# The last two GLA heads of a hybrid layer: matrix times activations first, then the value weights

## The chip, the cores and the metric

The kernel runs on one core of a Trainium2 chip. The metric is the device time of one launch in microseconds (us). The core has five engines that run side by side, each with an order of instructions fixed beforehand: TensorE (PE; its weight loads are listed as PEld), VectorE (DVE), ScalarE (ACT), GpSimd (POOL) and SyncE (SP), which here only issues transfers. They wait for one another by semaphores.

## The reference, cut to what matters

The layer works on 256 latent tokens and 256 context tokens of width 2048, in fp32. One input projection feeds windowed attention (16 query heads, 4 key heads), gated linear attention (GLA, 4 heads), and two gates. Only what the change touches:

```python
h = modulate(x, g_mix, shift, scale)     # rms_norm(x) * g * (1 + scale) + shift; the context likewise
qa, ka, va, qb, kb, vb, rb, lrf, lrb, gate_a, gate_b = split(h @ w_in)
# GLA, per head: a token's output is a sum over all tokens s, of latent and context,
#   o[t] = sum_s A[t, s] * vb[s]
# A comes from qb, kb and the decays alone; vb = h @ w_in[:, VB + 512*head : ...]
y_att = o_attn @ w_attn_o
y_gla = (rms_norm(o_gla, gla_norm) * silu(rb)) @ w_gla_o
x = x + mod * ((sigmoid(gate_a) * y_att + sigmoid(gate_b) * y_gla) @ w_out)
```

Since vb = h W, the output A vb can be formed as A (h W) or as (A h) W.

## The kernel before, in words

**Products.** Every large fp32 product is made of three fast ones: each factor is split into a high and a low part, and high × high, low × high and high × low are summed in a PSUM bank. `split` copies the high part on ACT (L62) and subtracts on DVE (L63). Weights stream as 512 KB pieces (two blocks of 128 rows by 512 columns) through SP's queue into seven `raw` buffers; `wsplit` splits each into `whi` (ACT, L220) and `wlo` (DVE, L221), three buffers each. A projection of 512 columns (`proj_nat`, `proj_T`) has eight such pieces. One piece costs TensorE 12 products of 512 columns where the 256 latent tokens alone are projected, and 24 for all 512 tokens.

**Order.** A scheduler fixes the order on each engine. In the code, `tick()` runs once a piece: it runs what `defer(n, ...)` put off by n pieces, advances a generator in `beside`, and runs steps of `bg_steps` at the rate `bg_rate`. Those steps make the later modulation vectors, each with one 512 KB load and one DVE instruction (L403).

**The stages that matter.** Four blocks with a GLA matrix beside them: `with_gla(h, ...)` runs `gla_A(h, ...)`, which yields the split matrices `ats` (latent) and `atc` (context), beside a block: the second half of the keys for head 0, the values of head 1, 2 and 3 (`v_block`, 192 products of 512 columns each) for the others. `gla_o(h, ...)` then multiplies matrix and values (24 products of 512 into `po`) and leaves the output in `og`, its sums of squares in `ssg`. For h > 0 `gla_A` uses split factors (`q2s`, `q3s`, `kk`) for the context's matrix, for h = 0 fp32 ones (`kf`, `kg`).

Then come attention's keys (KA) and values (VA) with `bg_rate` 1.6, and with `bg_rate` 0 the four query blocks (`qa_block`). `attend(g)` runs beside query block g + 1, the last one beside the first gate block (GA, into `m1`). In attention, `norm_rope` scales the queries by `rms_scale`, which is an Ln (L440) and an Exp (L441) on ACT with a Newton step on DVE around them (L442 to L445). Transposes put the queries into `ptq` and, split, into `qT`; `pS` holds scores, L1121 masks them into `s` and takes the maximum `mx`; the exponentials are transposed (`ptp`), split (`pth`, `ptl`) and multiplied by the values into `poa`. Banks `ptq`, `pS`, `ptp`, `poa`, `po` and others share a few PSUM banks, three of them "side" banks.

After attention `rg = rms_scale(ssg, ...)` scales the GLA outputs, four blocks `rb` are made with `bg_rate` 0.62, and the merge follows. Its Sigmoid of the gate `m1` (in `at_evac`, for j = 0, L1221) needs only `m1`. ACT computes a function from the table of a set that is loaded (ACT_TABLE_LOAD); early in the kernel a set that holds both Ln and Exp is loaded.

Of the kernel before, what the change touches and what calls it, by code (L numbers as in the profile page):

```python
# [32 lines left out]
def layer_kernel(ctx, tc, A, out):  # L33
# [27 lines left out]
    def split(hi, lo, src):  # L61
        S.activation(hi, src, AF.Copy)  # L62
        return V.tensor_tensor(lo, src, hi.bitcast(F32), op=ALU.subtract).ins  # L63
# [737 lines left out]
    def gla_A(h, kb, qb, R, gc, res):  # L801
# [44 lines left out]
        def products(lv, q2, k2):  # L846
            pa = bank("pa", (P, 2, P), side=True)
            for t in range(2):
                tq = t if lv < 7 else 1 - t
                for dt in range(2):  # L850
                    mm_b(pa[:, t, :], k2[:, dt, t * P:(t + 1) * P],
                              q2[:, dt, tq * P:(tq + 1) * P], start=(dt == 0), stop=(dt == 1))
            if lv < 7:
                V.copy_predicated(at, lmask[:, lv:lv + 1, :].to_broadcast([P, 2, P]), pa)
            else:
                split(ats[0][:, 0], ats[0][:, 1], at)
                split(ats[1][:, 0], ats[1][:, 1], pa)
# [187 lines left out]
    def norm_rope(b, r, t, tag, fold=None):  # L1045

        y = W2(tag, "y", [P, 4, P])
        S.activation(y, b.rearrange("p (h d) -> p h d", h=4), AF.Copy)
        sq = W2("fc", "sq", [P, 512])
        S.activation(sq, y.rearrange("p h d -> p (h d)"), AF.Square)  # L1050
        s4 = sm.tile([P, 4], F32, name="s4", tag="s4")
        V.tensor_reduce(s4, sq.rearrange("p (h d) -> p h d", h=4), op=ALU.add, axis=AX.X)
# [16 lines left out]

    kTh, kTl = M("kTh", [P, 4, 512], F32R), M("kTl", [P, 4, 512], F32R)  # L1070

    def ka_evac(i, b):
        z = norm_rope(b, rk if i < 2 else None, i % 2, "fa")

        def turn():
            pt = bank("ptk", (P, 4, P))
            for h in range(4):
                turn_b(pt[:, h, :], z[:, h, :], ident)
            split(kTh[:, :, i * P:(i + 1) * P], kTl[:, :, i * P:(i + 1) * P], pt)

        defer(2 + i, turn)
# [26 lines left out]
    def attend(g, qT, qr):  # L1108
        for t in range(2):
# [4 lines left out]
            for h in range(4):  # L1114
                qh, ql = (qT[:, i, h, t * P:(t + 1) * P] for i in range(2))
                pS = bank("pS", side=True)
                mm_b(pS, qh, kTh[:, g, :], start=True, stop=False)
                mm_b(pS, qh, kTl[:, g, :], start=False, stop=False)
                mm_b(pS, ql, kTh[:, g, :], start=False, stop=True)
                s_ = W2("fa", "s", [P, 512])  # L1120
                V.tensor_tensor_reduce(out=s_, in0=pS, in1=amask[:, t, :], scale=1.0, scalar=NEG,  # L1121
                                       op0=ALU.add, op1=ALU.max, accum_out=mx[:, h:h + 1])
                sc.append(s_)
# [42 lines left out]
    bg_rate[0] = 0.0  # L1166
    qTs = qa_block(0)
    m1 = [[W2("fc", "m1", [P, 512]) for _ in range(2)]]

    def ga_block():  # L1170
        proj_nat(w_in, 0, GA, ALL, h_x, lambda t, b: S.activation(m1[0][t], b, AF.Copy))

    for g in range(4):
        beside[:] = [attend(g, *qTs), 0.7, -2.9]
        qTs = qa_block(g + 1) if g < 3 else ga_block()
        for _ in beside[0]:
            pass
        beside.clear()
# [14 lines left out]
    for j in range(4):  # L1193
        def rb_evac(t, b, j=j):
# [278 lines left out]
```

## Time and profile before

| | |
|---|---|
| time, median of 3 runs | 1956.05 us (1956.04 to 1956.2) |
| time of the profiled execution | 1956.3 us, its span 1954.5 us |
| granted TensorE clock | 1.00 of full speed |
| transfers | 420.85 MB, mean 215 GB/s |
| ACT_TABLE_LOAD | 10, of 1283 ns |

A group in the profile reads: line, engine, operation, output<-inputs, shape, count; then busy time in us, mean ns of one; then the idle time of the engine just before. A timeline row reads: start in us, length in us, engine, line, operation, and in brackets the idle time before it with what ended it. A row of waits has total us, times, longest us.

### The profile page before, as it was taken

The numbers are of one execution on the slowest core, as the hardware profiler recorded it, in microseconds if no ns is written. First come the engines' busy times: TensorE is split into PE (matmuls) and PEld (weight loads), VectorE is DVE, ScalarE is ACT, GpSimd is POOL, SyncE is SP. The second block draws the span as 40 slices with busy tenths as digits, with TensorE's granted clock in tenths as the row PEclk, the third lists the DMA queues.
The fourth block names the chain that finished last, engine by engine and source line by source line (L and its number), as shares of the span: only waits on it lengthen the run. The fifth ranks groups of instructions, "written<-read, shape, count | busy, mean of one in ns | idle before, by whom it ended". The sixth has DMA issues, their size and how long they took to land.

```text
span 1954.5 us, 26414 instructions
## 1 busy us (share of the span) xinstructions
PE 1940.3 (99%) x9956; PEld 1612.6 (83%) x9956; DVE 1400.5 (72%) x2165; ACT 985.8 (50%) x1426; POOL 44.9 (2%) x60
## 2 busy tenths in 40 slices
PE   8999999999999999999999999999999999999999
PEld 6678888888887788888888888888888888888887
DVE  5756867785768898777775467998886555777754
ACT  5223666642355665444444445855555334655533
POOL 0010011110000000000000000000000000000000
PEclk9999999999999999999999999999999999999999
DMA  9984222236553467898987777688886666666663
GB/s 396 412 301 141 76 65 65 76 116 225 183 173 107 126 216 255 291 312 302 311 309 231 237 258 240 194 277 286 267 286 217 193 193 185 192 186 193 193 213 111
DMA packets 182576, 420.85 MB, mean 215 GB/s; under 512 B 12480, under 2 KB 12704, under 8 KB 177200
## 3 DMA queue, kind: packets, MB, share of 16 engines
q1 hardware_dynamic: 180912, 413.45, 64.8%
q0 software_dynamic: 1360, 5.54, 0.9%
q8 instruction: 78, 1.28, 0.3%
q14 instruction: 50, 0.41, 0.1%
q10 hardware_dynamic: 176, 0.17, 0.0%
HBM read 416.98 MB, written 2.13 MB: 214 GB/s over the span
## 4 chain that ended last, share of the span: by engine, by line
PE 96%; DMA 3%; ACT 1%; DVE 1%; issue 0%; POOL 0%; SPq 0%; ACTq 0%; DVEq 0%
PE acc L84 74%; PE accs L84 12%; PE pa L96 2%; PE poa L96 1%; PE pS L96 1%; PE po L96 1%; DMA mraw<-in_w_mod 1%; PE pm L96 1%; PE ptp L99 1%; DMA xr<-in_ctxT 1%; DMA raw<-in_w_in 1%; PE pto L99 0%; DMA pack<-in_k_pack 0%; PE plr L646 0%; PE ptx L99 0%; PE pr L491 0%
## 5 line engine op out<-in xcount | busy, mean ns | idle before, releaser
L220 ACT ACTIVATE whi<-raw 128x1024 fp32r<-128x1024 f32 x568 | 601.4, 1060 | 760.5 <-PE acc L84 594.5
L221 DVE TENSOR_TENSOR wlo<-raw,whi 128x1024 fp32r<-128x1024 f32 x568 | 693.4, 1223 | 399.7 <-ACT whi L220 386.1
L84 PE MATMUL accs<-h,whi 128*128 128x512 f32 x704 | 244.5, 392 | 0.0
L84 PE MATMUL acc<-h,whi 128*128 128x512 f32 x640 | 222.3, 392 | 0.0
L84 PE MATMUL accs<-h,wlo 128*128 128x256 f32 x704 | 196.0, 278 | 0.0
L84 PE MATMUL acc<-h,wlo 128*128 128x256 f32 x640 | 178.1, 278 | 0.0
L84 PEld LDWEIGHTS accs<-h,whi 128*128 128x128 f32 x704 | 131.8, 187 | 29.9
L84 PEld LDWEIGHTS acc<-h,whi 128*128 128x128 f32 x640 | 119.8, 187 | 27.0
L84 PE MATMUL acc<-whi,ah 128*128 128x512 f32 x352 | 137.1, 389 | 0.0
L84 PE MATMUL acc<-whi,al 128*128 128x512 f32 x352 | 137.0, 389 | 0.0
L84 PEld LDWEIGHTS accs<-h,wlo 128*128 128x128 f32 x704 | 132.5, 188 | 0.0
L84 PEld LDWEIGHTS acc<-h,wlo 128*128 128x128 f32 x640 | 120.5, 188 | 0.1
L84 PE MATMUL acc<-whi,h2hi 128*128 128x512 f32 x256 | 101.3, 396 | 0.0
L84 PE MATMUL acc<-whi,h1hi 128*128 128x512 f32 x256 | 100.8, 394 | 0.0
L84 PE MATMUL acc<-whi,h0hi 128*128 128x512 f32 x256 | 100.5, 392 | 0.0
L84 PE MATMUL acc<-whi,h0lo 128*128 128x512 f32 x256 | 100.2, 391 | 0.0
L84 PE MATMUL acc<-whi,h3hi 128*128 128x512 f32 x256 | 99.9, 390 | 0.0
L84 PE MATMUL acc<-whi,h1lo 128*128 128x512 f32 x256 | 99.9, 390 | 0.0
L84 PE MATMUL acc<-whi,h2lo 128*128 128x512 f32 x256 | 99.8, 390 | 0.0
L84 PE MATMUL acc<-whi,h3lo 128*128 128x512 f32 x256 | 99.7, 390 | 0.0
L84 PE MATMUL acc<-wlo,ah 128*128 128x512 f32 x352 | 94.2, 389 | 0.0
L403 DVE CUSTOM_DVE_ANT_0 raw<-raw,csrow,pack 128x1024 f32<-128x1024 f32 x64 | 81.3, 1280 | 0.0
(396 smaller groups left out, 3498.2 us busy)
## 6 DMA issues: line engine op xcount, KB each, us to landing
raw<-in_w_in SPq DMA_DIRECT2D x204, 512.0 KB, 4.6
raw<-in_w_up SPq DMA_DIRECT2D x176, 512.0 KB, 4.4
raw<-in_w_modT SPq DMA_DIRECT2D x128, 512.0 KB, 4.5
raw<-in_w_down SPq DMA_DIRECT2D x88, 512.0 KB, 3.7
mraw<-in_w_mod SPq DMA_DIRECT2D x32, 1024.0 KB, 14.0
raw<-in_w_attn_o SPq DMA_DIRECT2D x32, 512.0 KB, 5.2
raw<-in_w_gla_o SPq DMA_DIRECT2D x32, 512.0 KB, 5.7
raw<-in_w_out SPq DMA_DIRECT2D x32, 512.0 KB, 4.6
```

The costliest lines, as they stand in the source:

```text
L84: r = pe_seq(PE.matmul(*a, **k))
L96: return pe_seq(after(PE.matmul(*a, **k)))
L99: return pe_seq(after(PE.transpose(*a)))
L220: j = S.activation(hi[:, 0:n, :], raw[:, 0:n, :], AF.Copy).ins
L221: i = V.tensor_tensor(lo[:, 0:n, :], raw[:, 0:n, :], hi[:, 0:n, :].bitcast(F32), op=ALU.subtract).ins
L403: i0 = V.tensor_tensor_reduce(out=raws[i], in0=raws[i], in1=row[0], scale=1.0, scalar=d if h else bmod[:, b0:b0 + 1], op0=ALU.mult, op1=AL ...
```

## The change

Heads 2 and 3 no longer have value blocks. Their matrices form beside attention's values and keys, which are kept in fp32 (`va32`, `ka32`), and are kept split (`ax`, `ac`). The gate block (GA) moves ahead, with the norm, rotation and transposes of the keys put off into it. Then `pair_values` goes over the 2048 channels in eight pieces of 256. `natural(kp)` loads the tokens and the context again, in their natural layout, and modulates them with rows from a small DRAM buffer `drows` (four scalings and one addition on DVE, one addition on POOL, a split). `inner(kp)` multiplies them by both matrices into `pg` (24 products of 512) and splits that; `outer(kp)` multiplies by two 512 KB pieces of value weights (24 products) into four `acc` banks. The values' split (`values_split`) is put off into query block 0. `rg` is computed after query block 0, the first `rb` block runs beside the last attention in the gate block's place, and the later `bg_rate` is 0.75. Head 2 takes the fp32 path in `gla_A`.

```diff
@@ early, after the modulation
+    rcol = pack[:, 290:294]
+    pt = bank("ptr", (P, 4, P), side=True)
+    for i in range(4):
+        turn_b(pt[:, i, :], rrow1[i // 2][:, (i % 2) * P:(i % 2) * P + P], ident)
+    S.activation(rcol, pt[:, :, 0], AF.Copy)
+    def send_rows():
+        for i, col in enumerate((scale1, shift1)):
+            pt = bank("ptd", (2 * KT, P), side=True)
+            turn_b(pt, col.rearrange("p s k -> p (s k)"), ident)
...
+            G.dma_start(drows[2 * i:2 * i + 2, :].rearrange("s (k p) -> (s k) p", p=P), row)
@@ gla_A
-        if h:
+        if h % 2:
             kk = M("kk", [P, 2, 2, 2, T], F32R)
...
-    for h in (1, 2, 3):
-        a, v = with_gla(h, kb1 if h > 1 else kbt, lambda h=h: v_block(VB + h * 512, f"v{h}", h == 3))
-        if h < 3:
-            gla_o(h, a, *v)
-    defer(1, lambda: gla_o(3, a, *v))
+    defer(2, send_rows)
+    a, v = with_gla(1, kbt, lambda: v_block(VB + 512, "v1"))
+    gla_o(1, a, *v)
+    va32 = with_gla(2, kb1, lambda: kept(VA, "va32"))[1]
+    ka32 = with_gla(3, kb1, lambda: kept(KA, "ka32"))[1]
...
-    bg_rate[0] = 1.6
-    proj_nat(w_in, 0, KA, ALL, h_xc, ka_evac, by_tile=True)
-    vah, val = v_block(VA, "va", True)
+    def natural(kp):
+        raw = wr.tile([P, 4, T], F32, name="raw", tag="raw")
+        cols = slice(kp * 256, kp * 256 + 256)
+        for s, src in enumerate((A["x"], A["ctx"])):
+            load(raw[:, 2 * s:2 * s + 2, :], src[0][:, cols].rearrange("(t p) d -> p t d", p=P))
+        rows = wr.tile([P, 4, T], F32, name="rows", tag="raw")
+        load(rows, drows[:, cols].partition_broadcast(P))
+        for i in range(4):
+            V.scalar_tensor_tensor(raw[:, i, :], raw[:, i, :], rcol[:, i:i + 1], rows[:, i // 2, :],
+                                   op0=ALU.mult, op1=ALU.mult)
+            if i % 2:
+                x_ = raw[:, i - 1:i + 1, :]
+                (V if i == 3 else G).tensor_tensor(x_, x_, rows[...], op=ALU.add)
+        split(hh[e][:, 1], hl[e][:, 1], raw)
+    def pair_values():
+        banks = [acc.tile([P, 512], F32, name="acc", tag="acc") for _ in range(4)]
+        def inner(kp):
+            gb = [bank("pg", (P, 2, T), side=True) for _ in range(2)]
+            for n, (x_, y_) in enumerate(((0, 0), (0, 1), (1, 0))):
+                for k in range(2):
+                    for s in range(4):
...
+                        mm(gb[k], hn[x_][:, s, k * P:(k + 1) * P], m_, start=..., stop=...)
+            for k in range(2):
+                split(hh[2 + e][...], hl[2 + e][...], gb[k])
...
+        for kp in range(n + 1):
+            if kp + 1 < n and kp:
+                natural(kp + 1)
+            if kp < n:
+                inner(kp)
+            if kp:
+                for i in range(2):
+                    tick()
+                    outer(kp - 1, i, wsplit(w_in[r0:r0 + 2 * P, VB + (2 + i) * 512:VB + (3 + i) * 512]))
+    bg_rate[0] = 0.0
+    defer(2, lambda: natural(0))
+    defer(4, lambda: natural(1))
+    for i in range(4):
+        defer(10 + 3 * i, lambda i=i: keys(i))
+    proj_nat(w_in, 0, GA, ALL, h_x, lambda t, b: S.activation(m1[0][t], b, AF.Copy))
+    pair_values()
+    for i in range(4):
+        defer(1 + i, lambda i=i: values_split(i))
...
     qTs = qa_block(0)
+    rg = rms_scale(ssg, 512, [P, 4, 2])
...
+    for g in range(4):
+        beside[:] = [attend(g, *qTs), 0.7, -2.9]
+        qTs = qa_block(g + 1) if g < 3 else rb_block(0)
-    bg_rate[0] = 0.62
+    bg_rate[0] = 0.75
```

**What the scheduler makes of it.** In the rows below stand line, operation, output<-input and shape. First ACT around the end of the gate block GA: `m_...` are its two tiles, L1171 and L1214 copy them out of the bank, L1221 and L1356 are the Sigmoid. Before, beside the last attention:

```order
L1171 ACTIVATE m_4872<-acc 128x512
L1171 ACTIVATE m_4873<-acc 128x512
L62 ACTIVATE pth<-ptp 128x512
L1221 ACT_TABLE_LOAD
L1221 ACTIVATE m_4872<-m_4872 128x512
L62 ACTIVATE pth<-ptp 128x512
```

After, at the start of the pairs:

```order
L1214 ACTIVATE m_3910<-acc 128x512
L1091 ACTIVATE sq<-ka_3885 128x512 x4
L440 ACTIVATE rstd<-msq 128x4
L1356 ACT_TABLE_LOAD
L1356 ACTIVATE m_3909<-m_3909 128x512
L62 ACTIVATE h2hi<-pg 128x512 x2
L62 ACTIVATE h0hi<-raw 128x1024
L441 ACT_TABLE_LOAD
L441 ACTIVATE rstd<-rstd 128x4
L440 ACT_TABLE_LOAD
L440 ACTIVATE rstd<-msq 128x4 x3
L441 ACT_TABLE_LOAD
```

The Sigmoid moved with its gate block ahead of the keys' Ln and Exp, and these now have loads of their own. DVE at the same place after (L1134 and L1138 are the scalings and the addition of `natural`, L1093 the keys' sums of squares):

```order
L221 TENSOR_TENSOR wlo<-raw,whi 128x1024 x2
L1134 SCALAR_TENSOR_TENSOR raw<-raw,pack,rows 128x256
L1093 TENSOR_REDUCE s_4244<-sq 128x4
L1134 SCALAR_TENSOR_TENSOR raw<-raw,pack,rows 128x256
L439 TENSOR_SCALAR msq<-s_4244 128x4
L1134 SCALAR_TENSOR_TENSOR raw<-raw,pack,rows 128x256 x2
L1093 TENSOR_REDUCE s_4361<-sq 128x4
L1138 TENSOR_TENSOR raw<-raw,rows 128x512
L439 TENSOR_SCALAR msq<-s_4361 128x4
L1093 TENSOR_REDUCE s_4530<-sq 128x4
L1093 TENSOR_REDUCE s_4651<-sq 128x4
L63 TENSOR_TENSOR h2lo<-pg,h2hi 128x512 x2
```

The work of `natural` and of the keys stands here ahead of the first read of the `pg` banks; nothing of it stood at this place before.

Second, ACT from the end of query block 0 to attention 0, before and after (here `qT<-ptq` is the copy of the transposed queries):

```order
L220 ACTIVATE whi<-raw 128x1024
L440 ACTIVATE rstd<-msq 128x4
L441 ACTIVATE rstd<-rstd 128x4
L220 ACTIVATE whi<-raw 128x1024
L62 ACTIVATE qT<-ptq 128x4x128
L220 ACTIVATE whi<-raw 128x1024
L440 ACTIVATE rstd<-msq 128x4
L441 ACTIVATE rstd<-rstd 128x4
L62 ACTIVATE qT<-ptq 128x4x128
```

```order
L441 ACTIVATE rstd<-rstd 128x4
L62 ACTIVATE qT<-ptq 128x4x128
L440 ACT_TABLE_LOAD
L440 ACTIVATE rstd<-msq 128x4
L220 ACTIVATE whi<-raw 128x1024
L441 ACT_TABLE_LOAD
L441 ACTIVATE rstd<-rstd 128x4
L440 ACT_TABLE_LOAD
L440 ACTIVATE rstd<-msq 128x8
L441 ACT_TABLE_LOAD
L441 ACTIVATE rstd<-rstd 128x8
L62 ACTIVATE qT<-ptq 128x4x128
```

Each Ln and each Exp has a load ahead of it (the first pair, not shown, too), and the 8-wide ones of `rg` now stand here. DVE at that place, before and after:

```order
L445 TENSOR_TENSOR rstd<-rstd,newt 128x4
L63 TENSOR_TENSOR qT<-ptq,qT 128x4x128
L1067 TENSOR_SCALAR qr<-rstd 128x4
L1064 TENSOR_TENSOR sq<-sq,y 128x512
L442 TENSOR_TENSOR newt<-rstd 128x4
L1121 ISA s,mx<-pS,att 128x512
```

```order
L445 TENSOR_TENSOR rstd<-rstd,newt 128x4
L442 TENSOR_TENSOR newt<-rstd 128x4
L63 TENSOR_TENSOR qT<-ptq,qT 128x4x128
L1108 TENSOR_SCALAR qr<-rstd 128x4
L443 TENSOR_TENSOR newt<-newt,msq 128x4
L442 TENSOR_TENSOR newt<-rstd 128x8
L444 TENSOR_SCALAR newt<-newt 128x4
L221 TENSOR_TENSOR wlo<-raw,whi 128x1024
L445 TENSOR_TENSOR rstd<-rstd,newt 128x4
L443 TENSOR_TENSOR newt<-newt,msq 128x8
L1259 ISA s,mx<-pS,att 128x512
```

`newt` of the second token block moved ahead of the low half of `qT`, and the 8-wide `newt` and a `wlo` ahead of the first read of the scores (L1121 before, L1259 after).

Third, ACT in the first half of attention 0, before and after:

```order
L62 ACTIVATE pth<-ptp 128x512
L1050 ACTIVATE sq<-y 128x512
L1048 ACTIVATE y<-acc 128x512
L62 ACTIVATE pth<-ptp 128x512
L1050 ACTIVATE sq<-y 128x512
L62 ACTIVATE pth<-ptp 128x512
```

```order
L62 ACTIVATE pth<-ptp 128x512 x3
L440 ACT_TABLE_LOAD
L440 ACTIVATE rstd<-msq 128x4
L441 ACT_TABLE_LOAD
L441 ACTIVATE rstd<-rstd 128x4
L62 ACTIVATE pth<-ptp 128x512
```

The squares moved ahead, and between the last two `pth` an Ln and an Exp with their loads stand now.

More of the change, by code (lines that the diff above doesn't have):

```diff
@@ L777, in q_evac @@
         return eq
+    pair_x, pair_c = [], []
     def gla_gates(h):
@@ L854, in products @@
                 V.copy_predicated(at, lmask[:, lv:lv + 1, :].to_broadcast([P, 2, P]), pa)
-            else:
+            elif h < 2:
                 split(ats[0][:, 0], ats[0][:, 1], at)
                 split(ats[1][:, 0], ats[1][:, 1], pa)
-        ats = [W2("fc", "ats", [P, 2, 2, P], F32R) for _ in range(2)]
+            else:
+                split(pair_x[0][:, 0, h - 2, 0::3, :], pair_x[0][:, 1, h - 2, 0::3, :], at)
+                split(pair_x[0][:, 0, h - 2, 1:3, :], pair_x[0][:, 1, h - 2, 1:3, :], pa)
+        ats = [W2("fc", "ats", [P, 2, 2, P], F32R) for _ in range(2)] if h < 2 else None
+        if h == 2:
+            pair_x.append(M("ax", [P, 2, 2, 4, P], F32R))
         for lv in range(8):
@@ L917, in gla_A @@
                          stop=(n == len(parts) - 1 and dt == 1), skip_group_check=True)
-        atc = [W2("fc", "atc", [P, 2, T], F32R) for _ in range(2)]
-        split(atc[0], atc[1], pa)
-        res.extend((ats, atc))
+        if h < 2:
+            atc = [W2("fc", "atc", [P, 2, T], F32R) for _ in range(2)]
+            split(atc[0], atc[1], pa)
+            res.extend((ats, atc))
+            return
+        if h == 2:
+            pair_c.append(M("ac", [P, 2, 2, 2, T], F32R))
+        split(pair_c[0][:, 0, h - 2], pair_c[0][:, 1, h - 2], pa)
     def gla_o(h, a, vh, vl):
@@ L1068, in norm_rope, with keys @@
         return z
-    kTh, kTl = M("kTh", [P, 4, 512], F32R), M("kTl", [P, 4, 512], F32R)
-    def ka_evac(i, b):
-        z = norm_rope(b, rk if i < 2 else None, i % 2, "fa")
+    kT = []
+    def keys(i):
+        z = norm_rope(ka32[:, i, :], rk if i < 2 else None, i % 2, "fa", copied=True)
         def turn():
+            if not kT:
+                kT.extend(M(n, [P, 4, 512], F32R) for n in ("kTh", "kTl"))
             pt = bank("ptk", (P, 4, P))
@@ new lines, in pair_values, with outer, part0, part1 @@
+    def pair_values():
+        banks = [acc.tile([P, 512], F32, name="acc", tag="acc") for _ in range(4)]
+        def inner(kp):
+            e = kp % 2
+            hn = (hh[e][:, 1], hl[e][:, 1])
+            gb = [bank("pg", (P, 2, T), side=True) for _ in range(2)]
+            for n, (x_, y_) in enumerate(((0, 0), (0, 1), (1, 0))):
+                for k in range(2):
+                    for s in range(4):
+                        if s < 2:
+                            m_ = pair_x[0][:, y_, :, 2 * s:2 * s + 2, :].rearrange("p h b c -> p h (b c)")
+                        else:
+                            m_ = pair_c[0][:, y_, :, s - 2, :]
+                        mm(gb[k], hn[x_][:, s, k * P:(k + 1) * P], m_, start=(n == 0 and s == 0),
+                           stop=(n == 2 and s == 3))
+            for k in range(2):
+                split(hh[2 + e][:, 1, 2 * k:2 * k + 2, :], hl[2 + e][:, 1, 2 * k:2 * k + 2, :], gb[k])
+        def outer(kp, i, w):
+            e = kp % 2
+            hi, lo = w
+            gs = [g[2 + e][:, 1].rearrange("p (k h) t -> p k h t", h=2) for g in (hh, hl)]
+            def part0(t):
+                for k in range(2):
+                    for x_ in range(2):
+                        mm(banks[2 * i + t], gs[x_][:, k, i, t * P:(t + 1) * P], hi[:, k, :],
+                           start=(kp == 0 and k + x_ == 0), stop=False)
+            def part1(t):
+                for k in range(2):
+                    mm(banks[2 * i + t], gs[0][:, k, i, t * P:(t + 1) * P], lo[:, k, :], start=False,
+                       stop=(kp == KT // 2 - 1 and k == 1))
+            if kp == KT // 2 - 1:
+                for t in range(2):
+                    part0(t)
+                    part1(t)
+                    out_pair(i, t, banks[2 * i + t])
+                return
+            for part in (part0, part1):
+                for t in range(2):
+                    part(t)
+        def out_pair(i, t, po):
+            if len(og) < 2:
+                og.append(M("og2", [P, 2, 2, 512]))
+            S.activation(og[1][:, i, t, :], po, AF.Copy)
+            junk = W2("fb", "junk", [P, 512])
+            S.activation(junk, po, AF.Square, accum_out=ssg[:, 2 + i, t:t + 1])
+        n = KT // 2
+        for kp in range(n + 1):
[6 more added lines that the diff above has]
+                    tick()
+                    r0 = (kp - 1) * 2 * P
+                    outer(kp - 1, i, wsplit(w_in[r0:r0 + 2 * P, VB + (2 + i) * 512:VB + (3 + i) * 512]))
@@ new lines, in layer_kernel, with values_split @@
+    glan = att[:, 1536:2048]
+    m1 = [[W2("fc", "m1", [P, 512]) for _ in range(2)]]
+    bg_rate[0] = 0.0
[5 more added lines that the diff above has]
+    pair_values()
+    G.dma_start(glan, A["gla_norm"][0].partition_broadcast(P))
+    va = []
+    def values_split(i):
+        if not va:
+            va.extend(M(n, [P, 4, 512], F32R) for n in ("vah", "val"))
+        split(va[0][:, i, :], va[1][:, i, :], va32[:, i, :])
@@ L1116, in attend @@
                 pS = bank("pS", side=True)
-                mm_b(pS, qh, kTh[:, g, :], start=True, stop=False)
-                mm_b(pS, qh, kTl[:, g, :], start=False, stop=False)
-                mm_b(pS, ql, kTh[:, g, :], start=False, stop=True)
+                mm_b(pS, qh, kT[0][:, g, :], start=True, stop=False)
+                mm_b(pS, qh, kT[1][:, g, :], start=False, stop=False)
+                mm_b(pS, ql, kT[0][:, g, :], start=False, stop=True)
                 s_ = W2("fa", "s", [P, 512])
@@ L1141, in values @@
             def values(k, th, tl, low):
-                vk_h, vk_l = vah[:, k, g * P:(g + 1) * P], val[:, k, g * P:(g + 1) * P]
+                vk_h, vk_l = va[0][:, k, g * P:(g + 1) * P], va[1][:, k, g * P:(g + 1) * P]
                 first = mm_b(po, vk_h, th, start=(k == 0), stop=False)
@@ L1164, in attend @@
                   po.rearrange("p (a b) -> p a b", a=4))
-    bg_rate[0] = 0.0
     qTs = qa_block(0)
[L1168 to L1178, printed above, removed]
-    bg_rate[0] = 0.62
     rg = rms_scale(ssg, 512, [P, 4, 2])
-    gh = [M(f"gh{i}", [P, 8, T], F32R) for i in range(2)]
-    gl = [M(f"gl{i}", [P, 8, T], F32R) for i in range(2)]
+    gh, gl = [], []
     def to_T(src, hi, lo, j, t):
+        if len(hi) < 2:
+            hi.extend(M("th", [P, 8, T], F32R) for i in range(2))
+            lo.extend(M("tl", [P, 8, T], F32R) for i in range(2))
         pt = bank("pto", (P, 4, P), side=True)
@@ L1191, in to_T, with rb_block, rb_evac @@
         split(hi[j // 2][:, q4, t * P:(t + 1) * P], lo[j // 2][:, q4, t * P:(t + 1) * P], pt)
-    for j in range(4):
-        def rb_evac(t, b, j=j):
+    def rb_block(j):
+        def rb_evac(t, b):
             o_ = og[j // 2][:, j % 2, t, :]
@@ L1202, in layer_kernel @@
         proj_nat(w_in, 0, RB + j * 512, ALL, h_x, rb_evac)
+    for g in range(4):
+        beside[:] = [attend(g, *qTs), 0.7, -2.9]
+        qTs = qa_block(g + 1) if g < 3 else rb_block(0)
+        for _ in beside[0]:
+            pass
+        beside.clear()
+    bg_rate[0] = 0.75
+    for j in range(1, 4):
+        rb_block(j)
     def tok(hi, lo, t):
@@ L1209, in layer_kernel @@
     sig = []
-    mh = [M(f"mh{i}", [P, 8, T], F32R) for i in range(2)]
-    ml = [M(f"ml{i}", [P, 8, T], F32R) for i in range(2)]
+    mh, ml = [], []
     for j in range(4):
```

31 lines of the change are left out of this document (24 added, 7 removed).

## The prediction

> **What bounds the kernel now.** I read the page first: the busy shares, the chain that ended last, the costliest groups.
>
> ```profile
> span 1954.5 us, 26414 instructions
> PE 1940.3 (99%) x9956; PEld 1612.6 (83%) x9956; DVE 1400.5 (72%) x2165; ACT 985.8 (50%) x1426; POOL 44.9 (2%) x60
> PE 96%; DMA 3%; ACT 1%; DVE 1%; issue 0%; POOL 0%; SPq 0%; ACTq 0%; DVEq 0%
> L221 DVE TENSOR_TENSOR wlo<-raw,whi 128x1024 fp32r<-128x1024 f32 x568 | 693.4, 1223 | 399.7 <-ACT whi L220 386.1 <-PE acc L84 11.8 <-ACT ge L792 0.5
> ```
>
> TensorE is busy for 99% of the span and makes up 96% of the chain. So the time is TensorE's work plus the moments when it is made to wait, and any product removed is a gain unless a wait takes its place. The waits of TensorE come next, over the whole run (the largest row) and, for its weight loads, from 540 to 760 us, where attention runs; each row has total, times, longest.
>
> ```profile
> PE warm L572 <- DMA pack<-in_k_pack: 6.4, 1, 6.4
> PEld poa L96 <- DVE ptl L63: 2.2, 9, 0.3
> PEld ptp L99 <- DVE s L1136: 1.6, 7, 0.3
> ```
>
> The only long wait is the opening transfer. In attention its weight loads already wait in many short pieces, so that stage has little slack: what is made later on ScalarE (ACT) or VectorE (DVE) there is soon felt. The windows say which engine has room (length, then busy time of PE, PEld, DVE, ACT, POOL, then clock, DMA share, GB/s): attention beside the query blocks, attention's end beside the gate block, and the stages behind.
>
> ```profile
> 555.00:660.00 105.00, 104.75 (x495) 83.76 (x494) 86.52 (x201) 62.83 (x116) 0.00 (x0) 1.00 0.44 126
> 660.00:760.00 100.00, 99.98 (x472) 80.44 (x471) 90.57 (x175) 64.98 (x105) 0.00 (x0) 1.00 0.63 201
> 760.00:1050.00 290.00, 290.00 (x1303) 240.04 (x1301) 219.38 (x258) 125.69 (x130) 0.00 (x0) 1.00 0.89 301
> ```
>
> DVE works 82% to 91% of attention, ACT 60% to 65%. The granted clock is 1.00 in all of them.
>
> **The change part by part: TensorE's work.** In the projections one background step of twelve 512-wide products takes what ACT's rows show, five steps apart, when its `whi` split is let go by the products:
>
> ```profile
> 540.71 1.06 ACT L220 ACTIVATE whi<-raw 128x1024 fp32r<-128x1024 f32 x1 [1.66 <-PE acc L84]
> 554.31 1.06 ACT L220 ACTIVATE whi<-raw 128x1024 fp32r<-128x1024 f32 x1 [1.66 <-PE acc L84]
> ```
>
> 13.60 us for 60 products is 0.2267 us each. The two heads' value products go from 2 × 192 to 192 (the outer product over eight pairs, 24 for each head and pair), the 48 `po` products go, and 192 `pg` products come: 384 + 48 − 192 − 192 = 48 fewer, −10.9 us. Head 2 now takes its fp32 path, and six transposes come:
>
> ```profile
> L96 PE MATMUL pa<-q,kg 128*128 128x256 f32 x8 | 1.9, 379 | 0.0
> L96 PE MATMUL pa<-q3s,kk 128*128 128x256 f32 x36 | 4.8, 283 | 0.0
> L96 PE MATMUL pa<-q2s,kk 128*128 128x256 f32 x36 | 4.8, 283 | 0.0
> L99 PE MATMUL pto<-pack,sr 128*128 128x128 f32 x32 | 4.8, 272 | 0.0
> ```
>
> The one head that is fp32 now takes 1.9 us for `kg` and, with the same count and width, 1.9 for `kf`: 3.8; the three split ones 9.6 / 3 = 3.2; so +0.6 us. Six transposes at 4.8 / 32 = 0.15 are +0.9. TensorE's work: −10.9 + 0.6 + 0.9 = −9.4 us.
>
> **ACT's tables, the term against it.** The gate block's first pair of Sigmoids needs only `m1`. Its block now stands ahead of the pairs, and the order puts the Sigmoids there; the set that held both Ln and Exp is lost, and from then on each Ln and each Exp brings its own load: 33 loads in the order where before has 10. Of the 23 more, 5 stand at the start of the pairs, 6 between the first query block and the first attention, 4 in each of the next three query blocks. The price of one, at its place of before:
>
> ```profile
> 690.35 1.28 ACT L1221 ACT_TABLE_LOAD   x1
> 691.65 0.63 ACT L1221 ACTIVATE m<-m 128x512 f32<-128x512 f32 x1
> ACT whi L220 <- PE acc L84: 48.5, 28, 3.7
> ```
>
> 1.30 us from its start to the next instruction: 23 × 1.30 = 29.9 us of ACT. Bounds of what TensorE feels: nothing, if it all falls into the 48.5 us in which ACT waits for products between 540 and 760 us; 29.9 if none does. [...]
>
> I take neither end but walk the chain, first between query block 0 and attention 0, where the rows of before are:
>
> ```profile
> 558.52 0.19 ACT L440 ACTIVATE rstd<-msq 128x4 f32<-128x4 f32 x1
> 558.75 0.21 ACT L441 ACTIVATE rstd<-rstd 128x4 f32<-128x4 f32 x1
> 559.75 1.06 ACT L220 ACTIVATE whi<-raw 128x1024 fp32r<-128x1024 f32 x1 [0.80 <-PE acc L84]
> 561.85 0.60 ACT L62 ACTIVATE qT<-ptq 128x512 fp32r<-128x512 f32 x1 [1.04 <-PE ptq L99]
> 564.21 0.19 ACT L440 ACTIVATE rstd<-msq 128x4 f32<-128x4 f32 x1
> 564.43 0.21 ACT L441 ACTIVATE rstd<-rstd 128x4 f32<-128x4 f32 x1
> ...
> 563.73 0.68 DVE L63 TENSOR_TENSOR qT<-ptq,qT 128x512 fp32r<-128x512 f32 x1
> 565.00 0.15 DVE L442 TENSOR_TENSOR newt<-rstd 128x4 f32<-128x4 f32 x1
> 565.08 0.69 DVE L1121 CUSTOM_DVE_ANT_0 s<-pS,att 128x512 f32<-128x512 f32 x1
> ...
> 564.64 0.86 PE L96 MATMUL pS<-kTh,qT 128*128 128x512 f32 x3
> 566.03 0.39 PE L96 MATMUL pS<-kTh,qT 128*128 128x512 f32 x1
> ```
>
> ACT in the new order, on before's clock: load from 558.52, Ln 559.8, `whi` 560.05, load 561.0, Exp 562.3, `qT` 562.5, load 563.0, Ln 564.3, `whi` 564.5, load 565.5, Exp 566.8 (before 564.43). On DVE `newt` of the second token block, which needs that Exp, now stands ahead of `qT` (its low half), which so ends at 567.8 instead of 564.4. TensorE comes to the three score products that read it at about 565.3 (one 0.23 us step for each of three products that the order now puts ahead): it waits 2.5 us. Then ACT loads twice more for the 8-wide Ln and Exp of the GLA norm (`rg`, new at this place): Exp at 569.8, and on DVE its `newt` at 570.05, a `wlo` (1.22) and the first head's `s<-pS` follow, to 572.1. Only then is a side bank free for the fourth head's scores, which TensorE reaches at about 570.05: 2.0 us more. Together 4.5.
>
> In the first half of attention 0 the new order has an Ln and an Exp between the third and the fourth `pth`. Before has this pattern one attention later:
>
> ```profile
> 626.92 0.58 ACT L62 ACTIVATE pth<-ptp 128x512 fp32r<-128x512 f32 x1
> 627.40 0.19 ACT L440 ACTIVATE rstd<-msq 128x4 f32<-128x4 f32 x1
> 627.62 0.20 ACT L441 ACTIVATE rstd<-rstd 128x4 f32<-128x4 f32 x1
> 627.77 0.60 ACT L62 ACTIVATE pth<-ptp 128x512 fp32r<-128x512 f32 x1
> ...
> 629.04 0.39 PE L96 MATMUL poa<-pth,vah 128*128 128x512 f32 x1
> ```
>
> The product that reads the fourth came 629.04 − 628.37 = 0.67 us after its end; in attention 0 the new order has one product (0.23) less between, so 0.44 are left, and two loads of 1.30 make it 2.2 us late. In the second half of that attention the pair again stands ahead of all four `pth`, with a `whi` between; bounds nothing and 2.6, I take 2.1, as the place is nearest to this one. The four pairs of attentions 1 and 2 lie between nothing (the load at 690.35 stands in a window in which TensorE is busy 99.98 of 100 us) and 2.6; I take 1.5 each, nearer to the places I walked, as the same Ln and Exp stand there: 6.0.
>
> At the start of the pairs DVE is the late one, by these rows:
>
> ```profile
> L534 DVE SCALAR_TENSOR_TENSOR xr<-xr,scale,rrow 128x256 f32<-128x256 f32 x32 | 13.2, 479 | 0.1
> L1052 DVE TENSOR_REDUCE s<-sq 128x4 f32<-128x512 f32 x12 | 7.9, 679 | 0.7 <-ACT sq L1050 0.7
> L403 DVE CUSTOM_DVE_ANT_0 raw<-raw,csrow,pack 128x1024 f32<-128x1024 f32 x64 | 81.3, 1280 | 0.0
> 296.06 4.74 POOL L798 TENSOR_TENSOR gc<-gm,ge 128x256 f32<-128x256 f32 x1 [26.31 <-ACT ge L796]
> ```
>
> The second of two `wlo` needs the buffer that the gate block's last products read; with `whi` ahead of it, it ends about 0.9 + 1.22 = 2.1 us after the block. Then come four scalings (13.2 / 32 = 0.41), four reductions (7.9 / 12 = 0.66), an addition (half a `wlo`, 0.61) and two small ones (0.15): 2.1 + 1.64 + 2.64 + 0.61 + 0.3 = 7.3, and 0.7 for the low half of `pg`: at 8.0 us the first bank is free again. TensorE reaches the product that needs it after 24 + 7 products, 7.1 us: it waits 0.9. After that a pair gives DVE two `wlo` 2.45, two halves of `pg` 1.36, a split 1.22, scalings 1.7 and one addition 0.6: 7.3 us, under 48 × 0.2267 = 10.9 of TensorE. Between nothing and 2.6 (if the second bank too is a load late) I take 0.9, as all four reductions stand ahead in the order. A gain is excluded: no such wait stands there now.
>
> ```profile
> raw<-in_w_in SPq DMA_DIRECT2D x204, 512.0 KB, 4.6
> ```
>
> A pair brings, besides its two weight loads, 256 KB of the tokens, 256 KB of the context and 512 KB of rows through the same queue (SP) and the same seven `raw` buffers, of which it takes four in 10.9 us. A load lands in 4.6 us and is issued a pair ahead, so I cost it at nothing; if it came one landing late at the first pair only, 4.6 us. The rows' small writes on GpSimd's queue come two projection blocks earlier.
>
> Waits: 0.9 + 4.5 + 2.2 + 2.1 + 6.0 = 15.7. Some replace waits that stand there now; I take 2.5 of the 3.8 us quoted as such. 15.7 − 2.5 − 9.4 = +3.8 us. Against the profiled execution's own 1956.3 us that is 1960.1; its run lies 0.25 above the median of 1956.05, and the forecast in the median's terms is **1960 us**.
>
> The modulation steps that no longer run beside keys and values are made later, at 0.75 a step instead of 0.62. From 760 to 1050 us DVE is busy 219.38 of 290, 76%; 0.13 × 1.28 / 2.72 adds 6 points, and transfers grow by 1.75 / 1.62 from 301 to 325 GB/s, a DMA share of 0.89 × 1.75 / 1.62 = 0.96. DVE keeps room, and the share stays under one; I take nothing, where each per cent over one would cost 1 us in 100.
>
> **The rivals.** Within 0.2%, about 3.9 us, a measurement of this kernel can't be told from no change.
>
> *Loads hidden (faster).* ACT is idle 38% of attention, and the load at 690.35 cost TensorE next to nothing. If the products in the queue cover each pair of loads, and a load costs no more than the longest of the short waits quoted first, 0.3 us, 23 × 0.3 = 6.9 less the same 2.5: 1956.05 − 9.4 + 4.4 = 1951; with none felt, 1947. Against it: that load followed a `pth` that was not awaited, while at three walked places an awaited split stands behind two. It decides if half of the loads find 1.3 us of slack.
>
> *Balance.* Waits of three quarters of my sum, 11.8, with the same 2.5 off: 1956.05 − 9.4 + 9.3 = 1956; of half, 1952. The walk is least sure for attentions 1 and 2, so this is near.
>
> *The pairs wait for GpSimd (slower).* One of the two additions of a pair is on GpSimd (POOL) at 512 columns. Beside a DVE that never paused, 256 columns took 4.74 us; twice that, 9.5, plus scaling 0.8 and split 2.3 is 12.6 us against a pair's 10.9: 1.7 late in each of six pairs, +10, 1970. It decides at 7.8 us an addition. Against it: DVE pauses a third of a pair.
>
> [...]
>
> **How the numbers follow.** Forecast (1957.5 to 1966) 0.43; hidden 0.26; balance 0.18; GpSimd 0.09; drain 0.04. Faster by over 0.2% takes the hidden case and a part of balance, 0.30; within 0.2% the rest of balance and the forecast's lower third, 0.28; slower the rest, 0.42. For 8 in 10 the range holds all but the far ends of the outer cases: 1948 to 1970.
>
> **What the changed profile would show.** Some 48 fewer 512-wide products on TensorE; 33 loads on ACT; rows of TensorE waiting for `qT` and `pS` behind attention 0's start, each 2 to 3 us, and for `pth`; idle time of TensorE near the first `h2lo<-pg`, then none in the pairs; window of the pairs at about 10.9 us a pair. I am wrong if TensorE stays without gaps from the gate block to the end of attention (then 1948 to 1951), or if POOL's additions exceed 7.8 us with `hn` awaited.

## The result: 2003.57 us, 47 us slower

The changed kernel takes 2003.57 us (median of 6 runs, 1999.99 to 2004.8) against 1956.14 for the kernel before: a ratio of 1.0239, with a 95% interval of 1.0225 to 1.0252. The forecast was 1960, with a range up to 1970. Two launches beside the experiments, one of the kernel before (3686.5 us, granted clock 0.85) and one of run 11 (3239.2 us, 0.56), took far longer than the others of their kernel and are left out of all figures. From the page of the changed kernel: span, busy times, granted clock by fortieths of the span, and the chain by engine and by line.

```profile
span 2001.3 us, 26513 instructions
PE 1948.1 (97%) x9906; PEld 1612.8 (81%) x9906; DVE 1436.0 (72%) x2217; ACT 1026.5 (51%) x1468; POOL 58.1 (3%) x70
PEclk9999999997998999999999999999999999999999
PE 88%; DMA 5%; DVE 3%; ACT 3%; issue 1%; SPq 0%; DVEq 0%; ACTq 0%
PE acc L84 67%; PE accs L84 12%; DMA rows<-drows 3%; PE pa L96 2%; PE pg L84 1%; PE pS L96 1%; PE poa L96 1%; DVE wlo L221 1%; DMA mraw<-in_w_mod 1%; PE pm L96 1%; DVE raw L1134 1%; DMA xr<-in_ctxT 1%; DMA raw<-in_w_in 1%; ACT whi L220 1%; PE ptp L99 1%
```

TensorE's share of the chain fell from 96% to 88%; a transfer, `rows<-drows`, now holds 3% of it, some 60 us. And TensorE is busy 8 us longer (1948.1 against 1940.3) with less to do, at a granted clock of 0.991 where it was 1.00. TensorE is idle for 2001.3 − 1948.1 = 53.2 us, where before it was for 1954.5 − 1940.3 = 14.2. Two windows hold the 39 us that are new: the gate block's end and the pairs, and attention (columns as in the prediction).

```profile
400.00:560.00 160.00, 134.57 (x591) 109.41 (x590) 105.68 (x174) 66.42 (x101) 23.91 (x24) 0.93 0.53 138
600.00:770.00 170.00, 156.27 (x700) 121.66 (x699) 128.31 (x291) 113.17 (x182) 0.00 (x0) 0.96 0.40 118
```

Idle are 160 − 134.57 = 25.4 us in the first and 170 − 156.27 = 13.7 in the second. What TensorE waited for there (rows of the whole run, the largest of these two windows):

```profile
PE pg L84 <- DVE h2lo L63: 14.0, 2, 11.8
PE acc L84 <- DVE wlo L221: 9.3, 3, 5.1
PE poa L96 <- ACT pth L62: 7.2, 4, 1.9
...
PE pS L96 <- DVE qT L63: 2.2, 1, 2.2
PE ptp L99 <- DVE s L1274: 2.2, 1, 2.2
```

The first two are the pairs. The last three are attention: the prediction had walked waits for `pth` and `qT`, not the one for `s`. VectorE's own waits (380 to 560 us), the transfer's issue and landing, and the longest gap on the chain, in order of time:

```profile
DVE raw L1134 <- DMA rows<-drows: 42.3, 6, 9.0
rows<-drows SPq DMA_DIRECT2D x8, 512.0 KB, 8.9
...
473.16 2.35 DVE L221 TENSOR_TENSOR wlo<-raw,whi 128x1024 fp32r<-128x1024 f32 x2
484.50 0.48 DVE L1134 SCALAR_TENSOR_TENSOR raw<-raw,pack,rows 128x256 f32<-128x256 f32 x1 [9.00 <-DMA rows<-drows]
...
488.37 0.67 DVE L1138 TENSOR_TENSOR raw<-raw,rows 128x512 f32<-128x512 f32 x1
489.03 1.27 DVE L1093 TENSOR_REDUCE s<-sq 128x4 f32<-128x512 f32 x2
490.22 1.27 DVE L63 TENSOR_TENSOR h2lo<-pg,h2hi 128x512 fp32r<-128x512 f32 x2
490.95 1.22 PE L84 MATMUL pg<-ax,h1hi 128*128 128x512 f32 x2 [11.77 <-DVE h2lo L63]
```

VectorE stood 42.3 us in front of the scalings L1134 while rows of 512 KB took 8.9 us to land, and everything behind them in its order stood too: weight splits, and here the read that frees a `pg` bank. The loop closes on itself: the work held up is what releases the ring buffers, so the next transfer is issued late as well. SP waited 13.2 us, to 489.10, for the addition at 488.37 before it issued the next pair's loads. Two stretches of 2 us from the gap, and three after it, show the second loss:

```profile
480.00:482.00 2.00, 0.00 (x0) 0.00 (x0) 0.00 (x0) 0.00 (x0) 0.00 (x0) 1.00 1.06 79
486.00:488.00 2.00, 0.00 (x0) 0.00 (x0) 2.00 (x4) 1.88 (x3) 1.45 (x1) 0.50 0.07 25
492.00:494.00 2.00, 2.00 (x6) 1.61 (x5) 1.18 (x6) 1.97 (x5) 0.00 (x0) 0.50 0.13 38
494.00:496.00 2.00, 2.00 (x6) 1.52 (x6) 1.07 (x8) 1.81 (x5) 0.00 (x0) 0.50 0.42 87
498.00:500.00 2.00, 2.00 (x10) 1.65 (x10) 2.00 (x4) 1.99 (x4) 0.00 (x0) 1.00 0.76 81
```

During the gap the granted clock falls to 0.50, and when work returns it stays there for 5 to 6 us: 6 products start in 2 us instead of 10.

### The profile page after: what moved, and what is told of

The parts are those of the page before. It is cut to its first block, busy times and chain, and to the rows that moved or that the text cites. A ratio compares the mean times of both kernels' runs of the same rounds, so it can differ in the third digit from the quotient of the medians.

```text
span 2001.3 us, 26513 instructions
## 1 busy us (share of the span) xinstructions
PE 1948.1 (97%) x9906; PEld 1612.8 (81%) x9906; DVE 1436.0 (72%) x2217; ACT 1026.5 (51%) x1468; POOL 58.1 (3%) x70
## 4 chain that ended last, share of the span: by engine, by line
PE 88%; DMA 5%; DVE 3%; ACT 3%; issue 1%; SPq 0%; DVEq 0%; ACTq 0%
PE acc L84 67%; PE accs L84 12%; DMA rows<-drows 3%; PE pa L96 2%; PE pg L84 1%; PE pS L96 1%; PE poa L96 1%; DVE wlo L221 1%; DMA mraw<-in_w_mod 1%; PE pm L96 1%; DVE raw L1134 1%; DMA xr<-in_ctxT 1%; DMA raw<-in_w_in 1%; ACT whi L220 1%; PE ptp L99 1%
## 5 line engine op out<-in xcount | busy, mean ns | idle before, releaser
L84 PE MATMUL acc<-whi,th 128*128 128x512 f32 x256 | 100.5, 393 | 0.0
L84 PE MATMUL acc<-whi,tl 128*128 128x512 f32 x256 | 99.7, 389 | 0.0
L84 PE MATMUL acc<-whi,h1hi 128*128 128x512 f32 x224 | 89.2, 398 | 0.0
L84 PE MATMUL acc<-whi,h1lo 128*128 128x512 f32 x224 | 88.2, 394 | 0.0
L84 PE MATMUL acc<-whi,h0hi 128*128 128x512 f32 x224 | 88.2, 394 | 0.0
```

The source lines that it names most:

```text
L84: r = pe_seq(PE.matmul(*a, **k))
```

## The experiments

The theory to test: the loss is (a) the wait for the rows, made worse by VectorE's order, (b) the table loads in attention, (c) the half clock behind each gap. The rivals: the pairs are bound by VectorE's and GpSimd's own work; the lower clock belongs to the pairs' products; the loads are hidden.

**1. Late Sigmoid.**

```diff
-                S.activation(a1[t], a1[t], AF.Sigmoid)
+                in_order(last_hi[0], S.activation(a1[t], a1[t], AF.Sigmoid).ins)
```

> The changed kernel with one edit: the gate's first Sigmoid is ordered behind the weight splits of the merge, so that the set with Ln and Exp stays loaded and the order has 10 table loads again instead of 33. Theory: between 600 and 760 us of the changed kernel TensorE is idle for 13.7 us because of these loads, and the clock that is granted less after such gaps costs about 7 us more there; with the loads gone about 2003.6 - 20 = 1983 us. Rival A, the loads are hidden and the gaps come from the moved scalings and the new neighbours in the order: 2000 to 2004. The stall at the start of the pairs should stay in both.

Measured 1980.8 us, ratio to the kernel before 1.0123 (1.0106 to 1.0140). From 560 to 760 us TensorE is idle for 0.1 us:

```profile
560.00:760.00 200.00, 199.88 (x934) 161.13 (x934) 157.12 (x328) 119.84 (x209) 0.00 (x0) 1.00 0.45 143
```

The attention waits were the loads; the moved scalings cost nothing without them. TensorE is also busy 8.7 us less (1939.4 against 1948.1), with the same products: the lower clock behind those waits went with them (from 560 to 760 us 0.97 in the changed kernel, 1.00 here). From 400 to 560 us it still stands idle for 25.2 us.

**2. No row transfer.**

```diff
-        rows = wr.tile([P, 4, T], F32, name="rows", tag="raw")
-        load(rows, drows[:, cols].partition_broadcast(P))
+        rows = va32[:, 0:2, :].rearrange("p a (b c) -> p (a b) c", b=2)
```

> The changed kernel without the eight transfers of modulation rows: the scalings read a tile that lies in SBUF already, so the rows' values are left out of the result, and each pair takes three ring buffers instead of four. Theory: VectorE waits for these transfers 42.3 us in six pieces, with the weight splits queued behind it, and this is what leaves TensorE idle for about 23 us between 440 and 545 us and lowers its clock after it (about 10 us more): about 1970 us. Rival B, the pairs are bound by VectorE's and GpSimd's own work: TensorE stays idle there and the time falls by less than 10 us.

Measured 1975.57 us, 1.0096 (1.0081 to 1.0111). Of the pairs' waits 7.1 us for `h2lo` and 1.7 for a `wlo` remain. VectorE now waits 9.9 us for the activations' transfer at the same scalings: the theory holds for most of it, with a rest that it had not.

**3. Both.**

> Both edits together: Sigmoid late, no row transfers. If the two waits and the clock that follows them are the whole loss, the sum of TensorE's work remains: 1956 - 9.4 = 1947, with a few us of short waits 1947 to 1951, and a granted clock of 1.00 throughout. Rival C, the lower clock belongs to the products of the pairs themselves and not to the gaps: the clock stays near 0.991 and the time near 1960 or above.

Measured 1957.47 us, 1.0004 (0.9994 to 1.0013): neither expectation. The clock is 0.997, and what is missing are two waits of the pairs (and 1.1 us for a copy at 436.9 us), and the stretch of half clock behind the longer one; the last row is a window in the pairs after that stretch:

```profile
PE pg L84 <- DVE h2lo L63: 5.7, 1, 5.7
PE acc L84 <- DVE wlo L221: 1.7, 1, 1.7
...
480.00:500.00 20.00, 20.00 (x90) 16.57 (x89) 19.16 (x36) 7.62 (x10) 1.99 (x3) 1.00 0.48 146
```

So rival C falls, since the pairs' products behind that stretch run at full clock (1.00), but a third cause is left.

**4. Rows in pieces of 4 KB.**

```diff
-    drows = dram.tile([4, D], F32, name="drows")
+    drows = dram.tile([KT // 2, 4, 2, P], F32, name="drows")
...
-            G.dma_start(drows[2 * i:2 * i + 2, :].rearrange("s (k p) -> (s k) p", p=P), row)
+            for s in range(2):
+                for b in range(2):
+                    G.dma_start(drows[:, 2 * i + s, b, :], row[s * KT + b:(s + 1) * KT:2, :])
...
-        load(rows, drows[:, cols].partition_broadcast(P))
+        load(rows.rearrange("p a b -> p (a b)"), drows[kp].rearrange("r b p -> (r b p)").partition_broadcast(P))
```

> The changed kernel with the rows' DRAM buffer laid out by pairs, so that one partition reads its rows as one piece of 4 KB and not as four of 1 KB; the bytes and all else stay, the result too. If the number of pieces sets the landing (512 pieces of 1 KB took 8.9 us, 256 pieces of 2 KB of weights 4.4), 128 pieces land in about 3 to 5 us, each wait of VectorE shrinks by some 5 us and the time falls to about 1975 to 1990. If the broadcast's reading of one address or the late issue sets it, the landing stays at 8 to 9 us and the time at 2000 to 2005.

Measured 1981.36 us, 1.0126 (1.0111 to 1.0141). The landing halves, and so does VectorE's wait and more:

```profile
rows<-drows SPq DMA_DIRECT2D x8, 512.0 KB, 4.7
DVE raw L1136 <- DMA rows<-drows: 16.3, 6, 5.1
```

With the same bytes, a quarter of the pieces, each four times as large, landed in 4.7 us instead of 8.9.

**5. Late Sigmoid and 4 KB.** Edits 1 and 4.

> Late Sigmoid and rows in 4 KB pieces together, with the whole computation. If the two costs are independent the savings add: 2003.6 - 22.8 - 22.2 = 1958.6 us. Rival: with the loads gone VectorE's order at the start of the pairs changes and the rows' remaining waits (16.3 us) come to bear elsewhere: 1962 to 1970.

Measured 1960.22 us, 1.0018 (1.0008 to 1.0028). The savings add, within 2 us. One wait of 7.0 us for `h2lo` and 2.6 us for `wlo` are left, much as in run 3.

**6. The keys spread.**

```diff
-        S.activation(sq, b.rearrange("p h d -> p (h d)"), AF.Square)
+        first = S.activation(sq, b.rearrange("p h d -> p (h d)"), AF.Square)
+        if copied:
+            in_order(last_hi[0], first.ins)
```

> As the run before, and the norms of the four key tiles are ordered behind the weight splits of their own steps, so that they spread over the pairs instead of standing in a bunch at the start. Theory: what is left at the start of the pairs (5.7 us in the run without row transfers, 7.0 with 4 KB rows, and about 2 us at half clock behind it) is VectorE's and ScalarE's bunch of reductions, Ln and Exp ahead of the first reads of the banks; with them spread the wait falls to 2 to 4 us and the time to about 1954. Rival: the wait is natural's own (its transfer and four scalings ahead of the splits): unchanged within 2 us.

Measured 1960.04 us: no change; the wait for `h2lo` is 7.5 us. VectorE ahead of that read:

```profile
469.66 0.48 DVE L1138 SCALAR_TENSOR_TENSOR raw<-raw,pack,rows 128x256 f32<-128x256 f32 x1 [4.50 <-DMA rows<-drows]
...
474.85 0.68 DVE L63 TENSOR_TENSOR h2lo<-pg,h2hi 128x512 fp32r<-128x512 f32 x1
```

The saving that was forecast did not come, but the test is weaker than it was meant to be. VectorE still stands 4.5 us for the rows and then works 5.2 us up to the read, as in run 5 (5.3): reductions of later key tiles have gone, and the first tile's next steps have moved up into their place. So the transfer and the scalings do stand ahead of the read; that the keys have no part in the wait isn't shown.

**7. Scalings behind the split.** `natural` is cut into its loads and its scaling; the loads stay, the scaling goes behind the next pair's first weight split on VectorE, and the keys begin two steps later.

```diff
-            if kp + 1 < n and kp:
-                natural(kp + 1)
+            nat = natural_load(kp + 1) if kp + 1 < n and kp else None
...
-                    outer(kp - 1, i, wsplit(w_in[...]))
+                    w = wsplit(w_in[...])
+                    if i == 0 and nat is not None:
+                        natural_scale(*nat, behind=last_lo[0])
+                    outer(kp - 1, i, w)
```

> As the run before, and the scalings of a pair are ordered behind the next weight split on VectorE, while the transfers are issued where they were; the keys begin two steps later. Theory: what hurts is that VectorE waits for a transfer with the weight splits queued behind it; with the split ahead TensorE keeps its work: 1948 to 1952 us and a granted clock of 1.00. Rival: the scalings are now late for the next pair's first product, and TensorE waits there instead: 1955 to 1965.

The edits of runs 5 and 6 are in it too. Measured 1945.95 us (1945.87 to 1946.03), ratio 0.9946 (0.9931 to 0.9961): faster than both kernels, 10.7 us less than the kernel before beside it (1956.6). Its page and VectorE's wait for the rows:

```profile
span 1944.2 us, 26501 instructions
PE 1929.1 (99%) x9906; PEld 1604.0 (83%) x9906; DVE 1437.1 (74%) x2217; ACT 996.3 (51%) x1445; POOL 59.7 (3%) x76
DVE raw L1141 <- DMA rows<-drows: 0.9, 1, 0.9
```

TensorE has no wait in the pairs or in attention, and the granted clock is 1.00. VectorE's wait for the rows is 0.9 us where it was 42.3.

**8. A gap made on purpose in the kernel before.**

```diff
+            for _ in range(1 + extra.pop(0) if extra else 1):
-            i = V.tensor_tensor(lo[...], raw[...], hi[...].bitcast(F32), op=ALU.subtract).ins
+                i = V.tensor_tensor(lo[...], raw[...], hi[...].bitcast(F32), op=ALU.subtract).ins
...
+    extra[:] = [0, 0, 0, 10]
     qTs = qa_block(0)
```

> The kernel before with one gap made on purpose: in query block 0 one weight split on VectorE is done eleven times instead of once (11.4 us more on VectorE, same values), and nothing else changes. It measures what a gap costs beside its own length. Theory: TensorE waits about 9 us, and then works at half the granted clock for about 4 us, which costs 2 us more: 1956.1 + 11 = about 1967, with one short stretch of clock 0.50 behind the gap. Rival: the half clock in the changed kernel belongs to the pairs' products; then the clock stays at 1.00 and the time is gap alone, about 1965.

Measured 1968.33 us, 1.0061 (1.0046 to 1.0076): 11.7 us for a gap of 8.9.

```profile
PE acc L84 <- DVE wlo L223: 8.9, 1, 8.9
544.00:546.00 2.00, 0.00 (x0) 0.00 (x0) 1.97 (x2) 0.00 (x0) 0.00 (x0) 1.00 0.73 205
548.00:550.00 2.00, 0.00 (x0) 0.00 (x0) 1.97 (x2) 0.00 (x0) 0.00 (x0) 0.50 0.00 0
554.00:556.00 2.00, 2.00 (x6) 1.59 (x5) 1.23 (x1) 0.00 (x0) 0.00 (x0) 0.50 0.69 231
558.00:560.00 2.00, 2.00 (x11) 1.63 (x10) 0.97 (x1) 1.00 (x1) 0.00 (x0) 1.00 0.40 155
```

The products of the kernel before, behind a gap, ran at half clock too (0.50 from 554 to 556 us): it belongs to the gap, and cost 11.7 − 8.9 = 2.8 us on top of it.

**9. Scalings behind the split, alone in the changed kernel** (the edit of run 7 without the others).

> The changed kernel with one edit: the scalings of a pair are ordered behind the next weight split on VectorE (rows still in 1 KB pieces, Sigmoid still early, keys as changed). If the blocked queue was what made the slow transfer costly, the pairs' waits (23 us with about 10 us at half clock) go and the attention's stay: about 1972 us. Rival: a transfer that lands in 8.9 us is too late whatever the order, and half of the pairs' waits stay: 1985 or more.

Measured 1979.49 us, 1.0117 (1.0102 to 1.0132): 24 us come back, between the two expectations. One wait for `h2lo` remains. VectorE's and TensorE's rows, and what stands ahead of that wait:

```profile
DVE raw L1137 <- DMA rows<-drows: 5.3, 1, 5.3
PE pg L84 <- DVE h2lo L63: 6.8, 1, 6.8
...
464.76 1.06 ACT L220 ACTIVATE whi<-raw 128x1024 fp32r<-128x1024 f32 x1 [7.17 <-DMA raw<-in_w_in]
465.86 1.22 DVE L221 TENSOR_TENSOR wlo<-raw,whi 128x1024 fp32r<-128x1024 f32 x1 [4.00 <-ACT whi L220]
```

VectorE now waits for only one of the eight transfers, which land in 9.6 us: the first, long before the pairs (to 401.9 us), where no split stands ahead. The wait for `h2lo` has another cause here: a weight load lands late, so the weight split is late, and the scalings and the keys' reductions that stand behind it delay the read of the bank.

**10. The fastest version with 1 KB pieces.**

> The fastest version with its rows in 1 KB pieces again. It prices the pieces once the order on VectorE is right: if the order is enough, 1946 to 1949 us; if both are needed, 1953 to 1965, with TensorE waiting for a split of the pairs.

Measured 1956.6 us, 1.0001 (0.9991 to 1.0010): 10.7 us for the pieces; both are needed. Its gaps are 5.0 us for `h2lo` and, earlier, 2.1 for the last matrix of head 3 (`pa` behind `k`, L900). The earlier one is gone in run 7, where VectorE waits 0.9 us for the first transfer instead of 5.0. The later one follows a late weight load, as in run 9. Runs 10 and 7 differ by the pieces alone. The weights from 440 to 480 us, with the time from issue to landing, in run 10 and in run 7:

```profile
raw<-in_w_in SPq DMA_DIRECT2D x6, 512.0 KB, 9.0
raw<-in_w_in SPq DMA_DIRECT2D x8, 512.0 KB, 4.0
```

So the rows in 1 KB pieces cost more here than their own landing: the weights that share their queue took 9.0 us to land instead of 4.0.

**11. The fastest version with the early Sigmoid.**

> The fastest version with the Sigmoid early again: 35 table loads in the order instead of 10, all else kept. It prices the loads alone. My walk gave 14.8 us of waits behind the start of the pairs, the changed kernel showed 13.7 between 600 and 760 us, and 2 to 7 us of half clock come on top: 1946 + 14 + 4 = about 1964. Rival: most of it was due to the order and the late start, and the loads alone cost under 6 us: below 1952.

Measured 1965.69 us (three launches), 1.0044 (1.0028 to 1.0061): 19.7 us for 25 loads. Between the profiled executions, TensorE is idle 11.9 us more than in run 7 and busy 8.1 us longer (1937.2 against 1929.1). From 560 to 760 us it is idle 12.3 us:

```profile
560.00:760.00 200.00, 187.69 (x858) 148.11 (x857) 155.38 (x333) 131.39 (x208) 0.00 (x0) 0.98 0.44 143
```

## Why the prediction was wrong

*TensorE's work: −9.4 us, right within 2 us.* With these waits gone (run 7) the kernel is 10.7 us faster than before, and TensorE is busy 1940.3 − 1929.1 = 11.2 us less.

*The table loads: right in place and, as waits, in size, 14.8 us.* Attention's idle time in the changed kernel is 13.7 us, gone with the loads (run 1). The terms fit less well than their sum: the wait for `qT` is 2.2 us (walked 2.5), the fourth head's scores 0.8 (2.0), the two walked `pth` 1.9 and 1.5 (2.2 and 2.1), and what comes behind attention 0 is some 7 (6.0), so errors of about 1 us balance. Run 11 prices all loads at 19.7 us, of which 8.1 are TensorE working at a lower clock (0.98 against 1.00 from 560 to 760 us), which the sum had not. No run shows a drain, an unseen gap behind a load, to which the forecast gave a chance of 0.04: in the changed kernel the Exp behind the load at 490.17 us starts at 491.47, 1.30 us on.

*The step that failed: "A load lands in 4.6 us and is issued a pair ahead, so I cost it at nothing".* This is the largest error. I took the landing of the weights, 512 KB in 2 KB pieces, for a transfer in twice as many pieces of 1 KB: it landed in 8.9 us. And I asked only whether the bytes fit into a pair of 10.9 us, not what stands behind the first instruction that waits for them. On VectorE that was the weight splits and the reads of the `pg` banks, and these free the buffers without which the next transfer isn't issued (SP waits 84.1 us for `wlo` from 380 to 560 us). "None in the pairs" became 25.4 us of idle time (a gap of 1.9 us at 413.78 ahead of the pairs included), against 0.9 predicted. The work that I had put ahead of the first read of a bank (scalings, reductions, addition, small ones) was 5.2 us in my sum and 5.7 in the trace (484.50 to 490.22); what the sum had at nothing are the 9.0 us in front of it, in which VectorE stands for the rows. The fallback of 4.6 us, at the first pair only, was sized from the wrong row as well. Runs 4, 7, 9 and 10 show that the pieces and the order each carry a part, and that mending one alone is not enough: from the changed kernel, pieces alone give back 22.2 us, order alone 24.1.

*The term that was missing: the clock.* "The granted clock is 1.00 in all of them" was read from a kernel without gaps, and each wait was priced at its own length. TensorE is busy 1948.1 us in the changed kernel and 1929.1 in run 7, with the same 9906 products: 19.0 us of working at a lower clock (the profile's mean clock of 0.991 over 1948 us comes to 17.5). By runs 1 and 11 some 8 to 9 of them belong to the loads, so about 10 to the pairs. In the changed kernel and in run 8 the clock is 0.50 at the end of the gaps of 11.8 and 8.9 us, and stays there for some 5 us after work returns; it also fell behind a wait of 2.2 us (last section). These 19.0 us are 0.95% of the changed kernel's span, and 40% of this loss.

Together: 25.4 + 13.7 + 19.0 − 11.2 = 46.9 us, against 2001.3 − 1954.5 = 46.8 between the spans.

*The rivals.* Two rows of the changed kernel, the additions on GpSimd and a stretch of the later stages:

```profile
L1138 POOL TENSOR_TENSOR raw<-raw,rows 128x512 f32<-128x512 f32 x8 | 12.6, 1580 | 102.9 <-DVE raw L1134 75.8 <-DVE msq L439 14.9 <-ACT h3hi L62 12.2
...
1040.00:1080.00 40.00, 40.00 (x178) 33.15 (x177) 33.34 (x40) 16.50 (x17) 0.00 (x0) 1.00 0.95 339
```

GpSimd as the bound fell: an addition took 1.58 us where 7.8 was the point from which it decides, though that rival's 1970 lay nearer than my time. Hidden loads and the balance fell with run 1, as the loads' waits came to 13.7 of my 14.8 us. The later stages at 0.75 run at a DMA share of 0.95 with TensorE never idle, as costed.

*What stays open.* Run 6 moved the keys by order alone and run 7 delayed them by two steps as well; that delay wasn't tried by itself, and how much of the last wait for `h2lo` is the keys' work is open. Why some short gaps lower the clock and others do not wasn't tested: in the changed kernel the clock fell behind the wait of 2.22 us at 614.91 and stayed at 1.00 behind one of 2.19 at 709.72.

## What to carry to other kernels

Before costing a new transfer at nothing, take its landing from a row with the same size of piece, and then look up what is queued behind the first instruction that waits for it: VectorE, which waits in order, stood 42.3 us here and held up everything behind, the splits among it that free the very buffers the next transfer needs. Put work that waits for a transfer behind the work that feeds the bound engine, and make the pieces large (1 KB to 4 KB: 8.9 to 4.7 us), also for the sake of what shares the queue (the weights: 9.0 to 4.0 us). Where TensorE is the bound, price a wait of several us above its length (11.7 us here for a gap of 8.9), and keep functions of another table set away from alternating Ln and Exp (25 more loads cost 19.7 us here).

## What the runs showed of the hardware

A gap of 8.9 us in a stage at a clock of 1.00 cost 11.7 (run 8). A shorter gap lowered the clock too: behind a wait of 2.2 us for `qT` in attention of the changed kernel the clock was 0.57 from 616 to 624 us:

```profile
614.91 0.98 PE L96 MATMUL pS<-kTh,qT 128*128 128x512 f32 x3 [2.22 <-DVE qT L63]
616.00:624.00 8.00, 7.21 (x21) 5.24 (x20) 5.23 (x18) 2.64 (x4) 0.00 (x0) 0.57 0.22 66
```

A broadcast of the same 4 KB to 128 partitions landed in 8.9 us as 512 pieces of 1 KB and in 4.7 as 128 pieces of 4 KB (3.8 in run 7). With pieces of 1 KB (run 10) the 512 KB weight loads on the same queue took 9.0 us from 440 to 480 us, with pieces of 4 KB (run 7) 4.0.
